# A two-layer streaming encoder on one core: the kernel lays out its own instruction order, and the merge computes a group's factors at once

## The chip, the core and the metric

The kernel runs on one core of a Trainium2 chip. The metric is device time in microseconds (us) for one execution, and lower is better. The core has a matmul engine (PE, whose weight loads are listed as PEld), a vector engine (DVE), a scalar and activation engine (ACT), a general engine (POOL), and a queue that issues transfers (SP). Each engine takes its own instructions strictly in the order in which the built program lists them; an instruction whose inputs are not there holds back everything listed behind it on that engine.

## What is computed

Two layers, each one sub-layer with four groups of heads fed by one input projection:

```
aq, ak, av, ag, bcq, bckv, bkr, bg, cq, ck, cv, cg, mq, mg = split_in(rms(x) @ w_in)
o_a = band attention, 9 chunks of 64, relative bias, softmax
o_b = latent attention (low rank q and kv, rotary), softmax over the past
o_c = stick-breaking attention (sigmoids, reverse cumulative product)
o_m = attention into 256 memory tokens
y   = rms(heads(concat(o_a, o_b, o_c, o_m))) * out_g * silu(gates)
x   = x + y @ w_out
```

The prompt has 2048 frames of 1024 channels; a second input of 64 frames goes through the same layers with caches. All of it is float32.

## The kernel before

The 2048 frames are 16 tiles of 128 rows, and the sample is a 17th. They are worked in three blocks of 6, 6 and 5 tiles. Two streams of work are written as Python generators. The projection stream (`p_stream`) multiplies tiles by chunks of 256 weight columns: float32 operands are split into a high and a low part, and three matmuls per 128 rows of the contraction are summed (lines 404, 405 and 407, tile `pp`, from `xh`, `xl` and the weight pieces `wh`). A weight piece arrives by a transfer (`raw`), and POOL (line 306) and DVE (line 307) split it. The attention stream (`attention`) goes through units of one head and up to two query tiles: scores into `ps` (lines 857, 858, 860), a mask or a maximum on DVE, exponentials or sigmoids on ACT, for group C a scan on DVE (line 1104) and a product on POOL (line 1106), then transposes of the weights `s` into `pt` on PE (line 902), a split of `pt` into `ph` by ACT (line 905) and DVE (line 138), and the products `ot` with the values on PE (line 927). At the end `os`, `ob` and `opark` bring the output back to rows (lines 933, 943, 949).

The main loop at the end of `hybrid_step` decides, by a table of costs and due points (`target`), which of the two generators speaks next. That fixes the order in which instructions are written. It does not fix the order in which they run: the kernel is built in a context with `schedule_with_timeline_sim=True`, where the framework collects the written instructions, gives each tile one of the slots of its pool, and lists the instructions on each engine in an order of its own, by its own timing of them. On-chip sums share few slots: `pp` has two, the pool `ps_st` (for `ps`, `pt`, `ob` and the other transposes) five, `ot` one.

`merge` ends a group of one block. It takes the parked outputs `opark` (six tiles of 128 rows by four heads of 64) and works tile by tile: a square on ACT (line 1335), a sum over each head on DVE (line 1337), then for groups A, B and M a reciprocal of the softmax sums, two products and a scale-and-add on DVE (lines 1344 to 1347), a power of -0.5 on POOL (`rpow`, line 141, on 128x4 numbers), a product with the reciprocal on DVE (line 1351), the product with the output on DVE (line 1352), the product with the gate on POOL (line 1354), and a transfer to `Y`. For group C the small rows are one scale-and-add (line 1340) and the power. The output projection of the block reads `Y`.

```
            V.reciprocal(out=st[:, 1], in_=rs)
            V.tensor_tensor(out=st[:, 0], in0=st[:, 0], in1=st[:, 1], op=ALU.mult)
            V.tensor_tensor(out=st[:, 0], in0=st[:, 0], in1=st[:, 1], op=ALU.mult)
            V.tensor_scalar(out=st[:, 0], in0=st[:, 0], scalar1=1.0 / HD, scalar2=EPS, op0=ALU.mult, op1=ALU.add)
            rpow(st[:, 2], st[:, 0], nh)
```

Of the kernel before, what the change touches and what calls it, by code (L numbers as in the profile page):

```python
# [16 lines left out]
NH = 4  # L17
# [27 lines left out]

class PsumPool:
# [18 lines left out]
def hybrid_step(  # L65
# [15 lines left out]
    V, A, G, T = nc.vector, nc.scalar, nc.gpsimd, nc.tensor  # L81
# [18 lines left out]
    nc.sync.dma_start(out=ident_f[:, 0:128], in_=c_ident)  # L100
# [7 lines left out]
    def masks():  # L108
        for dst, src, w in ((bmask, c_bmask, 512), (spad, c_spad, 256)):
            raw = pj.tile([128, 512], F32, tag="kv", name="raw5", bufs=1)  # L110
            nc.sync.dma_start(out=raw[:, 0:w], in_=src)
            V.tensor_copy(dst, raw[:, 0:w])
        tri_f = pj.tile([128, 2, 128], F32, tag="nrm", name="tri_f", bufs=2)
        nc.sync.dma_start(out=tri_f[:, 0], in_=c_tri)
        nc.sync.dma_start(out=tri_f[:, 1], in_=c_stri)
# [52 lines left out]
    def layer_consts(l):  # L168
# [4 lines left out]
        nc.sync.dma_start(out=gc, in_=gcol[l])  # L173
        gr = lay.tile([128, NGAIN], F32, tag="gr", name="gr", bufs=1)
        nc.sync.dma_start(out=gr, in_=grow[l:l + 1, :].to_broadcast([128, NGAIN]))
# [6 lines left out]
        nc.sync.dma_start(out=qg, in_=qcol[l])  # L182
# [5 lines left out]
    def layer_weights(l):  # L188
# [6 lines left out]
        for k in range(2):  # L195
            raw = pj.tile([128, 512], F32, tag="kv", name="raw5", bufs=1)
            nc.sync.dma_start(out=raw[:, 0:384], in_=w_q[l, k * 128:(k + 1) * 128, :])
# [7 lines left out]
        nc.sync.dma_start(out=raw, in_=w_kv[l])  # L205
# [93 lines left out]
    def weights(job, c0, w, out):  # L299
# [14 lines left out]
        for k in range(0, 8, n):  # L314
            raw = pj.tile([128, n, 256], F32, tag="raw", name="raw", bufs=4)
            nc.sync.dma_start(out=raw[:, :, 0:w], in_=src[:, k:k + n])
# [126 lines left out]
    def folded(fn, w, t, pp, rstd):  # L443
# [8 lines left out]
        nc.sync.dma_start(out=up[:, 0:w], in_=ev[64:128, 0:w])  # L452
# [39 lines left out]
    def k_stack(src, dst, scale=None):  # L492
# [12 lines left out]
        nc.sync.dma_start(out=dst.rearrange("a (i p) t -> p (a i) t", p=128),  # L505
                          in_=kt.bitcast(F32).rearrange("p a i t -> p (a i) t"))

    def qr_stack(src, dst):
# [6 lines left out]
        nc.sync.dma_start(out=dst[0:2].rearrange("a p t -> p a t"), in_=kt.bitcast(F32))  # L515
        nc.sync.dma_start(out=dst[2], in_=kt[:, 0].bitcast(F32))

    def v_stack(src, dst):
# [4 lines left out]
        for a in range(2):  # L523
            nc.sync.dma_start(out=dst[a].rearrange("h p w -> p h w"),
                              in_=vs[64 * a:64 * a + 64].bitcast(F32).rearrange("p h a b -> p h (a b)"))

    def kr_stack(kr, dst):
# [10 lines left out]
        nc.sync.dma_start(out=dst, in_=kt.bitcast(F32))  # L538
# [27 lines left out]
    def load_trig(t):  # L566
        trig = pj.tile([128, 64], F32, tag="trig", name="trig", bufs=4)
        nc.sync.dma_start(out=trig, in_=c_trig[t * 128:(t + 1) * 128, :])
# [17 lines left out]
    def chunk_fns(l, b):  # L586
# [19 lines left out]
        def out_rows(t, prompt, sample, src):  # L606
            if t == SAMP:
                nc.sync.dma_start(out=sample, in_=src[0:64])
            else:
                nc.sync.dma_start(out=prompt, in_=src)  # L610
# [10 lines left out]
        def gate(g):  # L621
            def fn(t, pp, rstd):
# [6 lines left out]
                nc.sync.dma_start(out=d["G" + g, b][:, t - tl[0], :], in_=ev)  # L629
            return fn  # L630

        def ak(t, pp, rstd):
# [5 lines left out]
            if t == SAMP:  # L638
                nc.sync.dma_start(out=o_aks[l, 64:128, :], in_=nf[0:64])
            elif t >= NT - KEEP:  # L640
                nc.sync.dma_start(out=o_akp[l, rows(t - (NT - KEEP)), :], in_=nf)
            k_stack(nf, kdst("A", t))

        def av(t, pp, rstd):
            ev = evict(pp, rstd)
            yield
            if t == SAMP:
                nc.sync.dma_start(out=o_avs[l, 64:128, :], in_=ev[0:64])
# [920 lines left out]
```

## Time and profile before

| | |
|---|---|
| time, median of 3 runs | 3338.14 us (3336.03 to 3340.5) |
| the profiled execution's own time | 3338.43 us |
| its span, first to last instruction | 3336.3 us |
| PE, PEld busy | 3155.7 us (95%), 3012.4 us (90%) |
| DVE, ACT, POOL busy | 2658.4 us (80%), 1942.9 us (58%), 1509.3 us (45%) |
| matmuls | 24486 |
| transfers by the hardware queue | 554.10 MB, 58.7% of 16 engines |

The span is what the profile sees of one execution; its own time is 2.1 us longer. Busy time of an engine is the union of its instructions' durations. Matmuls overlap each other, so a busy PE is not necessarily a PE that issues as fast as it can.

### The profile page before, as it was taken

To read this page: it belongs to the slowest core of one execution; us is meant where nothing else is said; L and a number is where in the kernel's file an instruction comes from. 1 tells how busy PE (TensorE), PEld (TensorE's weight loads), DVE (VectorE), ACT (ScalarE), POOL (GpSimd) and SP (SyncE) were. 2 spreads that over 40 slices of the span, in tenths; PEclk is the share of its full clock that TensorE was granted. 3 is DMA by queue.
4 is the path that set the end of the run, shared out by engine and by line. 5 is a ranking of instruction groups with operands and counts; after the bars stand their busy time and mean duration, and the time that the engine had idled before them with its cause. 6 is when DMAs were issued, how large, how long until landed. Compare 5 with 4: busy or idle time off the path is not lost.

```text
span 3336.3 us, 75730 instructions
## 1 busy us (share of the span) xinstructions
PE 3155.7 (95%) x24486; PEld 3012.4 (90%) x24486; DVE 2658.4 (80%) x7977; ACT 1942.9 (58%) x5336; POOL 1509.3 (45%) x2353
## 2 busy tenths in 40 slices
PE   8999899999999998999999889999999999999998
PEld 7899899899998998999999788989998998989897
DVE  5686768999787689887777977799878888877984
ACT  4456645677665556565556765666646566654651
POOL 4554445566345246442434534466414444102553
PEclk9999999999999999999999999999999999999999
DMA  7655776545657666465566567654445766556644
GB/s 203 173 158 159 209 199 186 145 118 145 173 143 200 185 185 180 140 179 162 143 190 183 158 172 215 188 145 122 135 138 164 211 189 185 159 151 184 167 114 145
DMA packets 576122, 558.94 MB, mean 168 GB/s; under 512 B 70960, under 2 KB 478000, under 8 KB 575728
## 3 DMA queue, kind: packets, MB, share of 16 engines
q1 hardware_dynamic: 575728, 554.10, 58.7%
q8 instruction: 196, 3.21, 0.4%
q14 instruction: 198, 1.62, 0.2%
HBM read 378.21 MB, written 173.75 MB: 165 GB/s over the span
## 4 chain that ended last, share of the span: by engine, by line
PE 55%; DVE 18%; DMA 13%; issue 5%; ACT 4%; POOL 3%; SPq 2%; POOLq 0%; ACTq 0%; DVEq 0%
PE pp L405 10%; PE pp L404 10%; PE pp L407 9%; PE ot L927 6%; PE pt L902 6%; DVE wh L307 5%; DVE r L1104 3%; PE ps L857 3%; PE ps L858 3%; DVE ph L138 3%; PE ps L860 2%; PE ob L943 1%; DMA y<-y 1%; PE ptx L261 1%; PE ptk L496 1%
## 5 line engine op out<-in xcount | busy, mean ns | idle before, releaser
L405 PE MATMUL pp<-wh,xh 128*128 128x256 f32 x4416 | 1262.4, 290 | 14.1 <-DVE wh L307 13.5
L404 PE MATMUL pp<-wh,xh 128*128 128x256 f32 x4416 | 1256.5, 290 | 15.2 <-ACT ev L439 10.5
L407 PE MATMUL pp<-wh,xl 128*128 128x256 f32 (+1 forms) x4416 | 1245.9, 284 | 1.3 <-DVE xl L138 1.3
L405 PEld LDWEIGHTS pp<-wh,xh 128*128 128x128 f32 x4416 | 837.9, 190 | 37.7 <-DVE wh L307 25.3
L404 PEld LDWEIGHTS pp<-wh,xh 128*128 128x128 f32 x4416 | 834.4, 190 | 31.3 <-ACT ev L439 13.7
L407 PEld LDWEIGHTS pp<-wh,xl 128*128 128x128 f32 x4416 | 840.3, 191 | 11.8 <-DVE xl L138 2.3
L306 POOL TENSOR_SCALAR wh<-raw,gc 128x256 fp32r<-128x256 f32 (+1 forms) x848 | 470.4, 570 | 323.8 <-PE pp L407 160.2
L927 PE MATMUL ot<-ph,kv 128*128 128x256 f32 (+1 forms) x3104 | 588.9, 293 | 24.4 <-DVE ph L138 11.1
L905 ACT CAST ph<-pt 128x512 fp32r<-128x512 f32 (+2 forms) x840 | 450.7, 551 | 248.9 <-PE pt L902 233.7
L138 DVE TENSOR_TENSOR ph<-pt,ph 128x512 fp32r<-128x512 f32 (+2 forms) x840 | 525.9, 633 | 70.7 <-ACT ph L905 66.8
L902 PE MATMUL pt<-identr,s 128*128 128x128 f32 x3056 | 507.7, 275 | 24.2 <-ACT s L1001 7.8
L927 PEld LDWEIGHTS ot<-ph,kv 128*128 128x128 f32 x3104 | 454.4, 189 | 45.5 <-DVE ph L138 20.1
L307 DVE SCALAR_TENSOR_TENSOR wh<-raw,gc,wh 128x256 fp32r<-128x256 f32 (+1 forms) x848 | 467.6, 576 | 19.4 <-POOL wh L306 18.6
L1106 POOL TENSOR_TENSOR s<-s,r 128x512 f32<-128x512 f32 (+3 forms) x328 | 323.9, 988 | 343.0 <-DVE r L1104 293.6
L857 PE MATMUL ps<-kv,qbuf 128*128 128x512 f32 (+3 forms) x1024 | 377.2, 371 | 25.5 <-DVE r L1104 13.1
L902 PEld LDWEIGHTS pt<-identr,s 128*128 128x128 f32 x3056 | 360.0, 141 | 42.5 <-ACT s L1001 12.1
L141 POOL TENSOR_TENSOR st<-st,mhalf 128x4 f32<-128x4 f32 (+1 forms) x312 | 277.5, 896 | 256.0 <-DVE st L465 218.3
L1104 DVE TENSOR_TENSOR_SCAN r<-ps,r,one 128x512 f32<-128x512 f32 (+3 forms) x328 | 360.0, 1104 | 30.8 <-ACT ps L1097 28.4
L858 PE MATMUL ps<-kv,qbuf 128*128 128x512 f32 (+3 forms) x1024 | 350.5, 344 | 0.0
L439 ACT ACTIVATE ev<-pp,xst 128x256 f32<-128x256 f32 (+1 forms) x424 | 198.5, 470 | 160.0 <-PE pp L407 120.6
L1053 ACT ACTIVATE s<-s,nm 128x512 f32<-128x512 f32 (+3 forms) x328 | 212.6, 651 | 112.5 <-DVE nm L1045 66.0
L1094 ACT ACTIVATE s<-ps 128x512 f32<-128x512 f32 (+3 forms) x328 | 175.1, 534 | 145.7 <-DVE ps L1092 93.8
(172 smaller groups left out, 5072.7 us busy)
## 6 DMA issues: line engine op xcount, KB each, us to landing
raw<-in_w_in SPq DMA_DIRECT2D x288, 256.0 KB, 3.6
kv<-kvC SPq DMA_DIRECT2D x128, 256.0 KB, 4.2
kv<-kvB SPq DMA_DIRECT2D x128, 256.0 KB, 4.2
kv<-kvA SPq DMA_DIRECT2D x96, 256.0 KB, 4.4
raw<-in_w_out SPq DMA_DIRECT2D x96, 256.0 KB, 3.6
y<-y SPq DMA_DIRECT2D x136, 128.0 KB, 2.7
xin<-y SPq DMA_DIRECT2D x64, 256.0 KB, 3.9
qC<-kt SPq DMA_DIRECT2D x34, 256.0 KB, 2.7
```

Source lines behind the costliest of these rows:

```text
L138: (eng or V).tensor_tensor(out=dst, in0=src, in1=hi.bitcast(F32), op=ALU.subtract)
L306: G.tensor_scalar(out=h, in0=raw, scalar1=gc[:, k:k + 1], scalar2=1.0, op0=ALU.mult, op1=ALU.mult)
L307: V.scalar_tensor_tensor(out=lo, in0=raw, scalar=gc[:, k:k + 1], in1=h.bitcast(F32), op0=ALU.mult, op1=ALU.subtract)
L404: T.matmul(pp, lhsT=xh[:, k], rhs=wh, start=(k == 0), stop=False)
L405: T.matmul(pp, lhsT=xh[:, k], rhs=wl, start=False, stop=end)
L407: T.matmul(pp[:, 0:w], lhsT=xl[:, k], rhs=wh, start=False, stop=(k == 7))
L857: T.matmul(ps[:, 0:w], lhsT=q[:, 0, qs], rhs=kt[:, c0:c0 + w], start=True, stop=False)
L858: T.matmul(ps[:, 0:w], lhsT=q[:, 1, qs], rhs=kt[:, c0:c0 + w], start=False, stop=(qr is None))
L902: T.transpose(pt[:, (u + x) * 128:(u + x + 1) * 128], self.p_of(i, j), ident)
L905: A.copy(out=ph[:, 0:w], in_=pt[:, 0:w])
L927: T.matmul(ot[:, e * lo, il[0]:il[0] + n], lhsT=p["vt"](j), rhs=phl[:, e, u * 128:(u + n) * 128], start=start and e == 0, stop=stop and e ...
L1104: V.tensor_tensor_scan(r[:, 0:w][:, ::-1], cc[:, ::-1], one.to_broadcast([128, w]), r[:, w:w + 1], ALU.mult, ALU.min)
```

## The change

A class `Plan` stands between the kernel and the engines. Every call of an engine (and every transfer, now called through `Y`) is only recorded, in the order in which it was written, with the parts of tiles that it reads and writes. From these `Plan.add` finds what each instruction depends on. At the end `plan.issue` goes through all of them in a simulated time of its own: each engine takes, whenever it is free, the ready instruction that was written first, with a charge for its duration by kind and size (`cost`), a charge for the way from one engine to another (`LAG`), a charge for a change of the activation table, and with the pools' slots handed out in the order in which tiles were created. The instructions are then issued in the order of their simulated starts, in a context (`tc.manual_schedule()`) in which the framework keeps that order on each engine. The arithmetic, the tiles and the slot counts stay, but for the merge.

`merge` now has two passes over the tiles of a group: first all squares and sums, into one tile of 128 x (4 x 6 x 4), then the small rows once for all tiles (128x24, or 128x20 in the last block), and then the products, gates and transfers tile by tile.

```
+class Plan:
+    LAG = {"PE": 160, "DVE": 100, "ACT": 100, "POOL": 150, "SP": 200}
...
+        n = cols(outs[0])
+        if eng == "PE":
+            if method == "transpose" or kw.get("rhs") is None:
+                return 110, 271
+            n = cols(kw["rhs"])
+            return max(0.46 * n + 1, 110), 170 + 0.53 * n
+        if eng == "SP":
+            size = 4 * outs[0].shape[0] * n if len(outs[0].shape) > 1 else 4 * n
+            return 530, 2800 + size * 0.0072
+        if eng == "DVE":
+            if method == "tensor_tensor_scan":
+                d = 150 + 2.2 * n
+            elif n <= 16:
+                d = 185 + (cols(ins[0]) if method == "tensor_reduce" else 0) * 0.85
+            elif len(ins) > 1 and sbuf(ins[0]) and sbuf(ins[1]):
+                d = 200 + 1.35 * n
+            else:
+                d = 150 + 1.05 * n
+            return d - 80, d
+        if eng == "ACT":
+            d = 190 + 0.76 * n
...
+        elif kw.get("op") is not None and "pow" in str(kw["op"]):
+            d = 600 if n == 1 else 1050
+        elif method == "tensor_scalar":
+            d = 245 + 1.3 * n
+        else:
+            d = 200 + 1.75 * n
+        return d - 30, d
...
+            for e in ready:
+                while clock[e] <= now and ready[e]:
+                    i = heapq.heappop(ready[e])
+                    key = slot(i)
+                    if key is not None:
+                        parked[key].append(i)
+                        continue
...
+        with tc.manual_schedule():
+            for i in sorted(range(n), key=lambda i: (start[i], i)):
+                op = ops[i]
+                op[1](*op[2], **op[3])
...
-    V, A, G, T = nc.vector, nc.scalar, nc.gpsimd, nc.tensor
+    plan = Plan()
+    V, A, G, T, Y = [plan.engine(n, x) for n, x in (
+        ("DVE", nc.vector), ("ACT", nc.scalar), ("POOL", nc.gpsimd), ("PE", nc.tensor), ("SP", nc.sync))]
...
+        st = at.tile([128, 4, MAXB, NH], F32, tag="mst", name="mst", bufs=2)
         for i0 in range(nq):
+            y = at.tile([128, NH, HD], F32, tag="y", name="y", bufs=2)
+            A.activation(out=y, in_=opark[:, i0], func=ACTF.Square)
+            V.tensor_reduce(out=st[:, 0, i0], in_=y, op=ALU.add, axis=AX.X)
+            if i0 % 2 == 1:
+                yield
+        f0, f1, f2, sc = [st[:, i, 0:nq].rearrange("p q h -> p (q h)") for i in range(4)]
+        if g == "C":
+            V.tensor_scalar(out=f1, in0=f0, scalar1=1.0 / HD, scalar2=EPS, op0=ALU.mult, op1=ALU.add)
+            rpow(sc, f1, nq * nh)
+            yield
+        else:
+            V.reciprocal(out=f1, in_=rspark[:, 0:nq].rearrange("p q h -> p (q h)"))
+            V.tensor_tensor(out=f0, in0=f0, in1=f1, op=ALU.mult)
+            V.tensor_tensor(out=f0, in0=f0, in1=f1, op=ALU.mult)
+            V.tensor_scalar(out=f0, in0=f0, scalar1=1.0 / HD, scalar2=EPS, op0=ALU.mult, op1=ALU.add)
+            rpow(f2, f0, nq * nh)
+            yield
+            V.tensor_tensor(out=sc, in0=f1, in1=f2, op=ALU.mult)
+        for i0 in range(nq):
             gt = at.tile([128, 256], F32, tag="gt", name="gt", bufs=2)
...
+    plan.issue(tc)
```

The order on the engines, at three places. In the changed program every row has the line of `plan.issue`'s call, so the names of the tiles tell what a row is. The first place is DVE in the first layer, at the merge of the first group (C of the first block), before:

```order
L1337 TENSOR_REDUCE mst<-y 128x4 x2
L1340 TENSOR_SCALAR mst<-mst 128x4 x2
L1031 ISA s,mx<-ps,bmask 128x256
L1031 ISA mx 128x1
L1041 TENSOR_SCALAR nm<-mx 128x2
L1352 TENSOR_TENSOR y<-opark,mst 128x256
L627 SCALAR_TENSOR_TENSOR ev<-sg,ev 128x256
L1352 TENSOR_TENSOR y<-opark,mst 128x256
```

and of the changed program, the same merge behind its last sum:

```order
L291 TENSOR_REDUCE mst<-y 128x4 x2
L291 TENSOR_SCALAR mst<-mst 128x24
L291 TENSOR_TENSOR rspark<-rspark,f 128x2
L291 TENSOR_TENSOR rspark<-rspark,rst 128x2
L291 SCALAR_TENSOR_TENSOR ev<-sg,ev 128x256
L291 TENSOR_TENSOR y<-opark,mst 128x256 x2
L291 TENSOR_TENSOR ph<-pt,ph 128x512
```

The scale-and-add that releases the power on POOL, and the product that waits for it, stood once for each pair of tiles; now they stand once for all six, with three rows between them and a split of `ph` behind.

The second place is POOL at the same merge (`mst` with `mhalf` is the power, `wh` a weight piece), before:

```order
L141 TENSOR_TENSOR mst<-mst,mhalf 128x4 x2
L1354 TENSOR_TENSOR y<-y,gt 128x256 x2
L306 TENSOR_SCALAR wh<-raw,gc 128x256 x8
L141 TENSOR_TENSOR mst<-mst,mhalf 128x4 x2
L1354 TENSOR_TENSOR y<-y,gt 128x256 x2
```

and now:

```order
L291 TENSOR_SCALAR wh<-raw,gc 128x256 x8
L291 TENSOR_TENSOR mst<-mst,mhalf 128x24
L291 TENSOR_TENSOR y<-y,gt 128x256 x2
L291 TENSOR_SCALAR wh<-raw,gc 128x256 x8
L291 TENSOR_TENSOR y<-y,gt 128x256 x2
```

Three pairs of 128x4 powers became one of 128x24, and eight weight pieces that stood behind the first pair stand ahead of it.

The third place is PE in the second layer, group B of the second block, from the last transpose of a `pt` to the first product with the `ph` made from it, before:

```order
L902 MATMUL pt<-identr,s 128x128
L927 MATMUL ot<-ph,kv 128x256 x4
L943 MATMUL ob<-identr,os 128x128
L857 MATMUL ps<-kv,qbuf_89 128x512
L858 MATMUL ps<-kv,qbuf_89 128x512
L860 MATMUL ps<-kr,qr 128x512
L857 MATMUL ps<-kv,qbuf_89 128x512
L858 MATMUL ps<-kv,qbuf_89 128x512
L860 MATMUL ps<-kr,qr 128x512
L902 MATMUL pt<-identr,s 128x128 x2
L927 MATMUL ot<-ph,kv 128x256
```

and now:

```order
L291 MATMUL pt<-identr,s 128x128
L291 MATMUL ps<-kr,qr 128x512
L291 MATMUL ot<-ph,kv 128x256 x3
L291 MATMUL ps<-kv,qbuf_85 128x512 x2
L291 MATMUL ps<-kr,qr 128x512
L291 MATMUL pp<-wh,xh 128x256
L291 MATMUL ot<-ph,kv 128x256
```

Between the transpose and the product that needs its split stood 13 matmuls, and now stand eight.

## Rows read from the trace of the kernel before

**Rows 1.** The page: busy time of each engine, and the granted clock in 40 slices.
```profile
PE 3155.7 (95%) x24486; PEld 3012.4 (90%) x24486; DVE 2658.4 (80%) x7977; ACT 1942.9 (58%) x5336; POOL 1509.3 (45%) x2353
...
PEclk9999999999999999999999999999999999999999
```
**Rows 2.** Busy us by stretch: stretch, length, PE, PEld, DVE, ACT, POOL, clock, DMA, GB/s.
```profile
0.00:100.00 100.00, 82.61 (x589) 78.17 (x590) 55.60 (x190) 41.82 (x116) 43.66 (x96) 0.97 0.70 201
...
600.00:900.00 300.00, 287.17 (x2200) 271.22 (x2201) 271.08 (x671) 202.94 (x516) 169.28 (x253) 1.00 0.50 141
...
3200.00:3336.00 136.00, 120.64 (x951) 115.64 (x949) 81.27 (x162) 37.82 (x84) 53.69 (x79) 0.98 0.44 134
sum 3336.00, PE 3155.75 PEld 3012.37 DVE 2658.43 ACT 1942.95 POOL 1509.31; mean PE 242.75 PEld 231.72 DVE 204.49 ACT 149.46 POOL 116.10
```
**Rows 3.** Timeline of PE, a dense piece: start us, us, engine line operation.
```profile
1553.67 0.28 PE L405 MATMUL pp<-wh,xh 128*128 128x256 f32 x1
1553.79 0.28 PE L407 MATMUL pp<-wh,xl 128*128 128x256 f32 x1
1553.91 0.28 PE L404 MATMUL pp<-wh,xh 128*128 128x256 f32 x1
...
1556.23 0.40 PE L857 MATMUL ps<-kv,qbuf 128*128 128x512 f32 x1
1556.47 0.39 PE L858 MATMUL ps<-kv,qbuf 128*128 128x512 f32 x1
```
**Rows 4.** Groups of PE by form: xcount | busy us, mean ns | idle before, releasers.
```profile
L405 PE MATMUL pp<-wh,xh 128*128 128x256 f32 x4416 | 1262.4, 290 | 14.1 <-DVE wh L307 13.5
```
**Rows 5.** Waits of PE: who waited for whom, us in total, times, longest us.
```profile
PE pp L405 <- DVE wh L307: 13.5, 30, 1.6
PE ps L857 <- DVE r L1104: 13.1, 21, 2.1
...
PE ot L927 <- DVE ph L138: 11.1, 15, 2.1
...
PE pp L404 <- ACT ev L439: 10.5, 14, 2.5
...
PE pp L404 <- DVE fo L431: 0.2, 1, 0.2
```
**Rows 6.** Waits of all engines, the merge's power on POOL.
```profile
POOL mst L141 <- DVE mst L1347: 187.0, 36, 71.9
```
**Rows 7.** Groups of POOL by form.
```profile
L306 POOL TENSOR_SCALAR wh<-raw,gc 128x256 fp32r<-128x256 f32 x800 | 448.8, 577 | 307.3 <-PE pp L407 159.2 <-PE pp L405 101.8 <-issue 36.2
...
L141 POOL TENSOR_TENSOR st<-st,mhalf 128x4 f32<-128x4 f32 x210 | 220.4, 1052 | 182.1 <-DVE st L465 148.7 <-DVE mst L1346 8.5 <-DVE f L1048 5.0
L141 POOL TENSOR_TENSOR mst<-mst,mhalf 128x4 f32<-128x4 f32 x136 | 140.3, 1038 | 239.8 <-DVE mst L1347 187.0 <-DVE mst L1340 46.9 <-DVE nm L1041 3.8
...
L141 POOL TENSOR_TENSOR st<-st,mhalf 128x1 f32<-128x1 f32 x102 | 57.7, 573 | 73.9 <-DVE st L465 69.5 <-DVE rspark L1066 3.4 <-DVE nm L1041 0.2
```
**Rows 8.** Groups of DVE by form.
```profile
L138 DVE TENSOR_TENSOR ph<-pt,ph 128x512 fp32r<-128x512 f32 x616 | 416.2, 681 | 58.8 <-ACT ph L905 55.4
L1104 DVE TENSOR_TENSOR_SCAN r<-ps,r,one 128x512 f32<-128x512 f32 x224 | 283.4, 1273 | 16.4 <-ACT ps L1097 15.8
...
L1351 DVE TENSOR_TENSOR mst<-mst 128x4 f32<-128x4 f32 x102 | 23.4, 229 | 8.7 <-POOL mst L141 7.6 <-POOL r L1101 0.7
...
L1344 DVE RECIPROCAL mst<-rspark 128x4 f32<-128x4 f32 x102 | 17.0, 167 | 2.4 <-ACT s L1001 2.2
```
**Rows 9.** Groups of ACT by form.
```profile
L905 ACT CAST ph<-pt 128x512 fp32r<-128x512 f32 x616 | 354.1, 588 | 173.5 <-PE pt L902 168.5 <-PE ot L927 3.1
```
**Rows 10.** Timeline of all engines near the end: a split of `ph` handed from ACT to DVE.
```profile
3247.93 0.37 ACT L905 CAST ph<-pt 128x256 fp32r<-128x256 f32 x1 [1.67 <-DVE ph L138]
...
3248.33 0.42 DVE L138 TENSOR_TENSOR ph<-pt,ph 128x256 fp32r<-128x256 f32 x1
```
**Rows 11.** Timeline of all engines at a merge: DVE's rows, and PE's pause.
```profile
1236.19 1.05 DVE L1351 TENSOR_TENSOR mst<-mst 128x4 f32<-128x4 f32 x1
...
1237.28 0.67 DVE L1352 TENSOR_TENSOR y<-opark,mst 128x256 f32<-128x256 f32 x1
1237.87 0.68 DVE L138 TENSOR_TENSOR ph<-pt,ph 128x512 fp32r<-128x512 f32 x1
...
1238.61 0.74 PE L927 MATMUL ot<-ph,kv 128*128 128x256 f32 x4 [2.08 <-DVE ph L138]
```
**Rows 12.** Transfers of the page: KB each, median us from issue to landing.
```profile
kv<-kvC SPq DMA_DIRECT2D x128, 256.0 KB, 4.2
...
y<-y SPq DMA_DIRECT2D x136, 128.0 KB, 2.7
xin<-y SPq DMA_DIRECT2D x64, 256.0 KB, 3.9
```
**Rows 13.** Timeline at the last merge: PE's first transposes of the last projection, DVE's last output.
```profile
3255.46 1.03 PE L261 MATMUL ptx<-identr,xin 128*128 128x128 f32 x8
...
3255.91 0.23 DVE L949 TENSOR_TENSOR opark<-ob,opark 128x64 f32<-128x64 f32 x1 [0.76 <-ACT opark L948]
```

More of the change, by code (lines that the diff above doesn't have):

```diff
@@ L99, in hybrid_step @@
     ident_f = pj.tile([128, 256], F32, tag="ev", name="ident_f", bufs=3)
-    nc.sync.dma_start(out=ident_f[:, 0:128], in_=c_ident)
+    Y.dma_start(out=ident_f[:, 0:128], in_=c_ident)
     identr = const.tile([128, 128], F32R, name="identr")
@@ L204, in layer_weights @@
         raw = pj.tile([128, 512], F32, tag="kv", name="raw5", bufs=1)
-        nc.sync.dma_start(out=raw, in_=w_kv[l])
+        Y.dma_start(out=raw, in_=w_kv[l])
         copy_r(wkh, raw)
@@ L315, in weights @@
             raw = pj.tile([128, n, 256], F32, tag="raw", name="raw", bufs=4)
-            nc.sync.dma_start(out=raw[:, :, 0:w], in_=src[:, k:k + n])
+            Y.dma_start(out=raw[:, :, 0:w], in_=src[:, k:k + n])
             raws.append(raw)
@@ L451, in folded @@
         up = pj.tile([64, 256], F32, tag="up", name="up", bufs=1)
-        nc.sync.dma_start(out=up[:, 0:w], in_=ev[64:128, 0:w])
+        Y.dma_start(out=up[:, 0:w], in_=ev[64:128, 0:w])
         yield
@@ L537, in kr_stack @@
         A.copy(out=kt, in_=pt)
-        nc.sync.dma_start(out=dst, in_=kt.bitcast(F32))
+        Y.dma_start(out=dst, in_=kt.bitcast(F32))
     def small_T(src, n, tag):
@@ L567, in load_trig @@
         trig = pj.tile([128, 64], F32, tag="trig", name="trig", bufs=4)
-        nc.sync.dma_start(out=trig, in_=c_trig[t * 128:(t + 1) * 128, :])
+        Y.dma_start(out=trig, in_=c_trig[t * 128:(t + 1) * 128, :])
         return trig
@@ L607, in out_rows @@
             if t == SAMP:
-                nc.sync.dma_start(out=sample, in_=src[0:64])
+                Y.dma_start(out=sample, in_=src[0:64])
             else:
-                nc.sync.dma_start(out=prompt, in_=src)
+                Y.dma_start(out=prompt, in_=src)
         def q_norm(g):
@@ L628, in fn @@
                 yield
-                nc.sync.dma_start(out=d["G" + g, b][:, t - tl[0], :], in_=ev)
+                Y.dma_start(out=d["G" + g, b][:, t - tl[0], :], in_=ev)
             return fn
@@ L638, in ak @@
             if t == SAMP:
-                nc.sync.dma_start(out=o_aks[l, 64:128, :], in_=nf[0:64])
+                Y.dma_start(out=o_aks[l, 64:128, :], in_=nf[0:64])
             elif t >= NT - KEEP:
-                nc.sync.dma_start(out=o_akp[l, rows(t - (NT - KEEP)), :], in_=nf)
+                Y.dma_start(out=o_akp[l, rows(t - (NT - KEEP)), :], in_=nf)
             k_stack(nf, kdst("A", t))
@@ L647, in av @@
             if t == SAMP:
-                nc.sync.dma_start(out=o_avs[l, 64:128, :], in_=ev[0:64])
+                Y.dma_start(out=o_avs[l, 64:128, :], in_=ev[0:64])
             elif t >= NT - KEEP:
-                nc.sync.dma_start(out=o_avp[l, rows(t - (NT - KEEP)), :], in_=ev)
+                Y.dma_start(out=o_avp[l, rows(t - (NT - KEEP)), :], in_=ev)
             v_stack(heads(ev), vdst("A", t))
@@ L754, in f @@
             def f(x, q):
-                nc.sync.dma_start(out=x, in_=mem[i * 128:(i + 1) * 128, q * 512:(q + 1) * 512])
+                Y.dma_start(out=x, in_=mem[i * 128:(i + 1) * 128, q * 512:(q + 1) * 512])
             return f
@@ L768, in mv @@
             yield
-            nc.sync.dma_start(out=o_mvp[l, i * 128:(i + 1) * 128, :], in_=ev)
+            Y.dma_start(out=o_mvp[l, i * 128:(i + 1) * 128, :], in_=ev)
             v_stack(heads(ev), kv_part(d, "M", 1, i))
@@ L780, in load @@
             ev = pj.tile([128, 256], F32, tag="ev", name="ev", bufs=3)
-            nc.sync.dma_start(out=ev[:, 0:w], in_=src)
+            Y.dma_start(out=ev[:, 0:w], in_=src)
             return ev
@@ L1332, in merge @@
+        for i0 in range(nq):
             gt = at.tile([128, 256], F32, tag="gt", name="gt", bufs=2)
[L1333 removed]
+            Y.dma_start(out=gt, in_=d["G" + g, b][:, i0, :])
             y = at.tile([128, NH, HD], F32, tag="y", name="y", bufs=2)
[L1335 to L1337 removed]
```

273 lines of the change are left out of this document (219 added, 54 removed).

## The prediction

> **What bounds the kernel now.** I read the page first. PE is busy for 3155.7 of 3336.3 us, and its granted clock is 90% or more of the upper of its two levels, 2.4 GHz, in every slice [rows 1]; so the kernel is bound by PE, and what a change of order can give is the time in which PE does not issue. The page shows 3336.3 - 3155.7 = 180.6 us of it directly. DVE comes next with 80%, and in the stretch from 600 to 900 us with 271 of 300 us, next to PE's 287 [rows 2].
>
> Then I asked how dense a dense piece of PE is. In the timeline, matmuls of 256 columns follow each other every 0.12 us and those of 512 every 0.24 us [rows 3], while the group's mean duration is 290 ns [rows 4]: each overlaps the next ones, and busy time still counts the last 290 - 120 = 170 ns before every pause. The waits of PE are 63 kinds of 169.2 us in 224 pauses, the largest 13.5 us and the last 0.2 us [rows 5]. With the hidden tails the pauses cost 180.6 + 224 x 0.17 = 219 us. Of the idle time 17.4 us lie in the first 100 us and 15.4 us in the last 136 us [rows 2], where loads fill and the last projection drains. I leave these 33 us alone, and 186 us remain that a better order could reach.
>
> No kind dominates. Two of the four listed are data that come late (`wh`, `ph`: 24.6 us), the other two slots that a reader gives back late (the scan's `ps`, the eviction of `pp`: 23.6 us) [rows 5]. That is what it looks like when engines that work strictly in their listed order get a list that doesn't fit the durations of the chip. The plainest sign is POOL, which stood 187 us, once 71.9 us at a stretch, in front of the merge's power because it was listed long before DVE came to its input [rows 6].
>
> **The change part by part.**
>
> *The order.* Nothing that PE computes is added or removed: 24486 matmuls before and after. What counts is whether the planner's time is that of the chip. Its charges are, for the large kinds, within 2% of the rows: 119 ns against 0.12 us for a matmul of 256 columns [rows 3], 578 against 577 ns for a weight piece on POOL [rows 7], 688 against 681 ns for a split and 1276 against 1273 ns for a scan on DVE [rows 8], 579 against 588 ns for a cast [rows 9]. Ways between engines are charged above what they take: ACT to DVE 100 ns where the row shows 30 [rows 10], DVE to PE 160 where it shows 60 [rows 11]. A half of `kv` is charged 4.69 us where the median is 4.2 [rows 12]. So what PE waits for comes mostly a little earlier than planned. How much of the 186 us goes cannot be read from any row. It is bounded by nothing (every pause is a slot that stays full) and by all of it; a loss, with new pauses, is the first rival below. I take 70%, nearer to the upper end because data waits are half of the listed ones and many slots come free late only because their reader on DVE or ACT is listed late: **-130 us**.
>
> *The merge's small rows on DVE.* Outside group C there were 102 of each of five kinds, now 18: 84 x 5 rows of 167 to 229 ns [rows 8] are some 84 us of DVE. I cost them at nothing. PE is the bound, and DVE falls from 80 to about 77%; if PE became so dense that DVE were level with it, the 84 us would be part of what makes the 70% possible.
>
> *The power on POOL.* 136 of 1038 ns become 24, of 24 columns (16 times) or 20 (8 times). A power of one column takes 573 ns, of four 1052 [rows 7]: 160 ns a column over 413 ns. At that slope 24 columns take 4.25 us and 20 take 3.6; the ends are 1.05 us, if the width costs nothing, and 6.3 us, if it is six times four. I take the slope, since both rows lie on it. POOL then spends 97 us instead of 141, but the planner charges 1.05 us whatever the width, so each power ends about 3 us after its plan. Behind it on DVE stands the product that needs it: in the built order 1 to 21 rows lie between the scale-and-add and that product, five or fewer in 14 of the 24 merges, at most some 1.8 us of cover. DVE then stands for 4.25 - 1.8 = 2.5 us, with splits of `ph` queued behind it, in 14 places: 35 us. The row at 1237 us shows the way of it today: the merge's rows stand ahead of a split on DVE, and PE pauses 2.08 us for that split [rows 11]. PE has projection matmuls listed between, so I pass on half: **+18 us**, between 0 and 60. On POOL itself weight pieces or group C's products stand behind some powers; they are late by the same 3 us and are within this bound.
>
> By the Trainium skill (GPSIMD Engine Reference, 3.1, Elementwise) an operation with two inputs costs about 2.6 cycles per element on POOL, so that the width would be almost free; as an estimate from that page the power would stay near 1.1 us, this term would be nothing, and the sum 18 us lower. The rows speak against it for a power: three more columns cost 479 ns [rows 7].
>
> *Chains with little cover.* From the last transpose of a `pt` to the product with its `ph` PE has work listed; by the spacing of rows 3 it is under 1.7 us for 98 of the 840 in the new order, for 26 in the old. The chain itself takes 588 + 30 + 681 + 60 ns = 1.36 us [rows 8 to 11] and the transposes' own tail. So up to 72 more chains fall short by up to 0.4 us, at most 29 us. The planner could have put projection work there if any had been ready; many of them lie in the last block's group C. I take **+8 us**.
>
> *The last merge.* The sums of all five tiles come before the one power. From the last output at 3256 us [rows 13] the way is a square, a sum, 3.6 us of power, a product, the gate, 2.7 us of writing and 3.9 us of reading [rows 12], together some 12.5 us, so the last projection can start near 3269; before, its first transposes came at 3255.5 [rows 13]. Covered or not depends on the projection that is left over: in the new order the last attention product stands 220 matmuls (26 us at 0.12) earlier in PE's list, which is cover enough. I take **+5 us**, between 0 and 13.
>
> *SP and transfers.* The same transfers go out, in planned order too. A store that waits for a late result holds the loads behind it, as now. I count no gain and no loss.
>
> **Sum.** 3338.4 (the profiled execution, 0.3 us over the median of the runs) - 130 + 18 + 8 + 5 = **3239 us**.
>
> **The rivals.**
>
> *Slower: every chain pays.* The planner gives PE an attention product as soon as its inputs should be ready. If on the chip DVE is late for the splits as a rule, because its rows stretch while POOL works (the merge's product took 1.05 us at 1236 us against a mean of 229 ns [rows 8, 11]), PE pays at each of the 840. At 0.25 us each that is 210 us; even with all of the 186 us gone, and the other terms' 31 us, the result is 3338 - 186 + 210 + 31 = 3393. It is slower from 0.18 us a chain on. For it speaks the shorter cover in the third place of the order, eight matmuls instead of 13; against it, that the planner's charges leave the chain some 0.27 us more than the rows take. Chance 0.11.
>
> *No change: the slots are full.* Five slots for `ps`, `pt` and `ob`, two for `pp`, one for `ot` are what they were. If PE's pauses are times in which no slot is free in any order, they come back elsewhere: 3338. The Trainium skill (Perfetto Trace Analysis, Optimization Strategy) says that the same gap repeating on the engine that should be saturated can mean too few buffers; by that rule an order gives nothing. The trace bears it out for about half of the listed waits, and no single gap repeats: 63 kinds share 169 us [rows 5]. Chance 0.06, with the case that a small gain is just eaten by the power.
>
> *Nearly all pauses go.* If 95% go and the width of the power costs nothing, it is 3338 - 177 + 5 = 3166; with 85% it is 3338 - 158 + 5 = 3185. Chance 0.2.
>
> *The change does not do what it says.* The built program's order differs on every engine in the way the change describes, so this gets no chance of its own.
>
> **How the numbers follow.** My own case, with 50 to 85% of the pauses gone, has 0.48 and by itself lies between 3200 and 3275. A smaller gain (5 to 50%, or the bounds of the other terms at their worst) has 0.15, up to 3331. With the third rival that makes 0.83 for faster by over 0.2% (6.7 us, about what a measurement of this kernel can tell from no change), 0.06 for no change, 0.11 for slower. The range runs from 3165, where nearly all of the third rival is in, to 3330; left out are no change and slower, 0.17.
>
> **What would show it.** PE idle on the page at 90 to 130 us instead of 180.6, and the waits view with fewer than 150 pauses. POOL's group of the 128x24 power at 4.2 us, and DVE waiting for it in some 14 merges. POOL no longer standing for tens of us in front of a merge. The forecast is wrong if the power shows 1 us (then the sum is 18 us too high), if `ot` waiting for `ph` grows to more than 100 us (the first rival), or if waits for slots keep their sum while the others vanish (the second).

## The result, and the profile after

The changed kernel takes **3284.4 us** (median; 3282.2 to 3298.25) where the kernel before took 3339.3 beside it: a ratio of 0.9845, 95% interval 0.9817 to 0.9874, so 1.3 to 1.8% faster. In microseconds that is -52 by the ratio and -55 by the medians, where the forecast was 3239, -99.

First the page of the changed kernel, which answers to [rows 1]: busy time and granted clock.

```profile
PE 3144.2 (96%) x24486; PEld 3007.0 (92%) x24486; DVE 2623.8 (80%) x7529; ACT 1954.2 (60%) x5336; POOL 1467.9 (45%) x2241
...
PEclk9999999999999999999999999999999999999999
```

The span is 3281.8 us, so PE's idle time went from 180.6 to 137.6 us, and 11.5 us of its busy time went too. The hidden tails of the prediction, 0.17 us behind each of the 62 pauses that are gone, would be 10.5 of them. The clock is as before, 0.992 of its upper level on average against 0.991. DVE lost 34.6 us of busy time, not 84: neighbouring rows overlap ([rows 11]: the split at 1237.87 starts 0.08 us before the product ahead of it ends), so a short row that goes frees less than its duration.

Next the waits of PE, changed kernel (who waited for whom, us in total, times, longest us), for [rows 5]:

```profile
PE pp L291 <- DVE wh L291: 11.3, 27, 0.9
PE ptx L291 <- DMA xin<-in_x_prompt: 9.7, 5, 6.5
PE pp L291 <- ACT ev L291: 9.2, 8, 4.0
PE ot L291 <- DVE ph L291: 8.0, 9, 1.8
PE pt L291 <- POOL s L291: 6.2, 8, 1.8
PE ps L291 <- DVE r L291: 6.1, 12, 1.1
...
PE ot L291 <- DVE r L291: 0.2, 1, 0.2
```

59 kinds share 124.8 us in 162 pauses; before it was 63, 169.2 and 224. The four kinds listed there all shrank, the scan's most (13.1 to 6.1). What has grown is the fifth row, where PE waits for a product on POOL: 6.2 us, before 1.1 in two pauses. All of PE's waits for POOL rose from 3.6 to 12.7 us.

The merge's power, groups by form on POOL, DVE and ACT of the changed kernel, for [rows 7], [rows 8] and [rows 9] (xcount | busy us, mean ns | idle before, releasers):

```profile
L291 POOL TENSOR_TENSOR st<-st,mhalf 128x4 f32<-128x4 f32 x210 | 224.0, 1069 | 206.1 <-DVE st L291 171.2 <-DVE nm L291 25.4 <-DVE f L291 4.3
...
L291 POOL TENSOR_TENSOR mst<-mst,mhalf 128x24 f32<-128x24 f32 x16 | 66.9, 4182 | 70.2 <-DVE mst L291 70.2
L291 POOL TENSOR_TENSOR st<-st,mhalf 128x1 f32<-128x1 f32 x102 | 57.5, 572 | 99.3 <-DVE st L291 67.1 <-DVE nm L291 21.3 <-DVE rspark L291 10.4
...
L291 POOL TENSOR_TENSOR mst<-mst,mhalf 128x20 f32<-128x20 f32 x8 | 28.3, 3539 | 27.4 <-DVE mst L291 22.1 <-DMA y_p<-xr 4.6 <-DVE r L291 0.7
```
```profile
L291 DVE TENSOR_TENSOR ph<-pt,ph 128x512 fp32r<-128x512 f32 x616 | 413.7, 682 | 110.4 <-ACT ph L291 107.5
L291 DVE TENSOR_TENSOR_SCAN r<-ps,r,one 128x512 f32<-128x512 f32 x224 | 280.8, 1269 | 20.2 <-ACT ps L291 19.6
```
```profile
L291 ACT CAST ph<-pt 128x512 fp32r<-128x512 f32 x616 | 355.8, 588 | 200.8 <-PE pt L291 193.6 <-DVE xr L291 2.9 <-DVE r L291 0.7
```

The power of 24 columns takes 4.18 us, of 20 columns 3.54: the slope of 160 ns a column, which gives 4.25 and 3.61, holds to about 2% far outside the two widths from which it came. Splits, scans and casts cost what they did. And DVE stands for the power, in the waits of all engines, for [rows 6]:

```profile
POOL mst L291 <- DVE mst L291: 92.3, 16, 24.2
...
DVE mst L291 <- POOL mst L291: 35.3, 15, 3.1
...
DVE y L291 <- POOL mst L291: 8.1, 4, 2.7
```

Where the pauses went by stretch, windows of the kernel before and then of the changed one (stretch, length, PE, PEld, DVE, ACT, POOL, clock, DMA, GB/s), beside [rows 2]:

```profile
0.00:600.00 600.00, 559.84 (x4395) 541.85 (x4396) 428.01 (x1361) 319.76 (x929) 300.68 (x521) 0.99 0.65 185
600.00:3000.00 2400.00, 2288.25 (x17719) 2177.95 (x17720) 1979.90 (x6048) 1472.23 (x4064) 1069.21 (x1634) 0.99 0.59 165
3000.00:3400.00 400.00, 307.66 (x2375) 292.56 (x2373) 250.51 (x568) 150.96 (x344) 139.43 (x198) 0.98 0.45 128
```
```profile
0.00:600.00 600.00, 561.83 (x4371) 539.50 (x4372) 434.67 (x1314) 326.10 (x942) 301.20 (x507) 0.99 0.66 185
600.00:3000.00 2400.00, 2316.17 (x18062) 2216.48 (x18061) 1976.32 (x5796) 1498.53 (x4107) 1038.96 (x1559) 0.99 0.60 169
3000.00:3400.00 400.00, 266.22 (x2057) 251.01 (x2055) 212.82 (x421) 129.54 (x289) 127.74 (x176) 0.99 0.37 105
```

PE's idle time is the length less the first number (in the last stretch, what is left of the span). It goes from 40.2 to 38.2 us in the first 600 us, from 111.7 to 83.8 in the middle, and from 28.6 to 15.6 at the end (336.3 - 307.7 and 281.8 - 266.2). The start hardly gained. (The stretches are cut by time, and the faster kernel is a little further on at each cut.) The waits of PE in the first 600 us of the changed kernel begin so:

```profile
PE ptx L291 <- DMA xin<-in_x_prompt: 9.7, 5, 6.5
PE pp L291 <- ACT ev L291: 8.4, 6, 4.0
```

At the other end, the last projection's first transposes, for [rows 13], in PE's timeline:

```profile
3199.03 0.49 PE L291 MATMUL ptx<-identr,xin 128*128 128x128 f32 x3
...
3206.34 0.60 PE L291 MATMUL ptx<-identr,xin 128*128 128x128 f32 x4
```

They carry no bracket: PE did not stand in front of them, as it had projection matmuls to issue.

### The profile page after: what moved, and what is told of

The parts are those of the page before. It is cut to its first block, busy times and chain, and to the rows that moved or that the text cites. A ratio compares the mean times of both kernels' runs of the same rounds, so it can differ in the third digit from the quotient of the medians.

```text
span 3281.8 us, 75026 instructions
## 1 busy us (share of the span) xinstructions
PE 3144.2 (96%) x24486; PEld 3007.0 (92%) x24486; DVE 2623.8 (80%) x7529; ACT 1954.2 (60%) x5336; POOL 1467.9 (45%) x2241
## 5 line engine op out<-in xcount | busy, mean ns | idle before, releaser
L291 PE MATMUL pp<-wh,xh 128*128 128x256 f32 (+1 forms) x9104 | 1811.1, 292 | 29.1 <-DVE wh L291 11.3
L291 PEld LDWEIGHTS pp<-wh,xh 128*128 128x128 f32 x9104 | 1439.2, 190 | 69.1 <-DVE wh L291 26.4
L291 PE MATMUL ot<-ph,kv 128*128 128x256 f32 (+1 forms) x3232 | 577.1, 289 | 14.4 <-DVE ph L291 8.0
L291 PE MATMUL ps<-kv,qbuf 128*128 128x256 f32 (+3 forms) x2048 | 543.5, 361 | 25.8 <-DVE r L291 6.1
L291 ACT ACTIVATE s<-s,nm 128x512 f32<-128x512 f32 (+4 forms) x600 | 383.9, 642 | 189.1 <-DVE nm L291 181.7
L291 DVE SCALAR_TENSOR_TENSOR wh<-raw,gc,wh 128x256 fp32r<-128x256 f32 (+1 forms) x848 | 476.5, 596 | 24.8 <-POOL wh L291 24.2
L291 PEld LDWEIGHTS ot<-ph,kv 128*128 128x128 f32 x3232 | 463.6, 190 | 29.1 <-DVE ph L291 11.6
L291 PEld LDWEIGHTS ps<-kv,qbuf 128*128 128x128 f32 x2048 | 321.5, 190 | 54.9 <-DVE r L291 11.0
L291 ACT ACTIVATE s<-ps 128x512 f32<-128x512 f32 (+3 forms) x328 | 166.1, 538 | 99.8 <-DVE ps L291 56.7
L291 DVE TENSOR_SCALAR_CACHE_REDUCE s<-ps 128x512 f32<-128x512 f32 (+1 forms) x328 | 181.5, 573 | 29.3 <-PE ps L291 28.8
L291 ACT COPY os<-ot 128x256 f32<-128x256 f32 (+1 forms) x384 | 139.4, 363 | 97.1 <-PE ot L291 95.0
```

What stands on the lines that cost most here:

```text
L291: op[1](*op[2], **op[3])
```

## The experiments

The theories. **A**: the term for the wide power was right, and the planner, which charges 1.05 us for it, sets rows behind it too early. **B**, in the first four runs: DVE's stops are covered, and what is missing is missing in the order itself. **S, D, P**, and B in the last run: ways in which the order could give less than 70%, namely, one for each, slots of `wh`, rows that run late against the plan, the choice of the oldest ready row, and banks of PSUM. **C**: the batched merge is itself worth something. Every kernel below is compared with the kernel before on its own chip, by the ratio; the first four shared one chip.

### The changed kernel again

No edit.

> The changed kernel once more, on the chip of the next three, so that they can be set against it. Both theories: 3280 to 3290 us, 0.981 to 0.987 of the kernel before.

Measured: 3288.5 us, 0.9849 (0.9829 to 0.9869). The result stands, and this is the value that the next three are set against.

### The power charged by its rows

```
-            d = 600 if n == 1 else 1050
+            d = 413 + 160 * n
```

> The plan charges the power 413 + 160 n ns for n columns (4.25 us for 24, 3.6 us for 20, 1.05 us for 4) instead of 1.05 us; nothing else differs. Theory A (the term of 18 us for the power is right: DVE's stops behind the power reach TensorE): the 35.3 us for which DVE waits behind the power fall below 8 us, and the time falls by 10 to 18 us against the changed kernel. Theory B (the pauses that stayed come from the order itself; DVE's stops are covered by what the cores of the pipeline hold ready): DVE's waits fall all the same, and the time stays within 5 us of the changed kernel.

Measured: 3263.9 us, 0.9769 (0.9749 to 0.9789). One line of the planner gives 24.6 us against the changed kernel, more than A's 10 to 18, and B's "within 5" falls. From the waits of this kernel:

```profile
DVE mst L291 <- POOL mst L291: 4.5, 4, 3.0
...
DVE y L291 <- POOL mst L291: 3.8, 3, 2.3
```

DVE's stops went from 35.3 + 8.1 to 8.3 us in all, while the power itself is as long as it was (4185 ns). How a stop reached PE is to be seen in the changed kernel. Timeline at 2124 us, all engines (start us, us, engine line operation, in brackets the idle time before and its end):

```profile
2124.07 4.16 POOL L291 TENSOR_TENSOR mst<-mst,mhalf 128x24 f32<-128x24 f32 x1
...
2128.26 0.18 DVE L291 TENSOR_TENSOR mst<-mst 128x24 f32<-128x24 f32 x1 [2.57 <-POOL mst L291]
...
2130.06 0.69 DVE L291 TENSOR_TENSOR ph<-pt,ph 128x512 fp32r<-128x512 f32 x1
...
2130.80 0.63 PE L291 MATMUL ot<-ph,kv 128*128 128x256 f32 x3 [1.77 <-DVE ph L291]
```

DVE stands 2.57 us, a split of `ph` runs after what was held up, and PE stops 1.77 us for it. That is the way that the prediction described. There is a second way, on POOL, at 629 us:

```profile
629.52 4.17 POOL L291 TENSOR_TENSOR mst<-mst,mhalf 128x24 f32<-128x24 f32 x1
...
633.66 1.08 POOL L291 TENSOR_TENSOR s<-s,r 128x512 f32<-128x512 f32 x1
633.72 1.06 DVE L291 TENSOR_TENSOR mst<-mst 128x24 f32<-128x24 f32 x1 [2.48 <-POOL mst L291]
...
634.80 0.55 PE L291 MATMUL pt<-identr,s 128*128 128x128 f32 x3 [1.85 <-POOL s L291]
```

Group C's product `s` stands behind the power on POOL itself, and PE waits for that product, not for DVE. That is the row of PE's waits that grew to 6.2 us; with the true charge it is 3.2. DVE stands for a power over 1 us long in 18 places of the changed kernel; PE pauses within 4 us of the end of 14 of them, 20.3 us in all, by going through the timeline stop by stop. Some of these would have fallen there anyway.

### The order alone, and the merge alone

The first is the changed kernel with the old merge, tile by tile (its loop as in the code before, with `Y.dma_start`, and `mst` in eight slots of 128x4). The second is the kernel before, in the framework's order, with the new merge.

```
-        st = at.tile([128, 4, MAXB, NH], F32, tag="mst", name="mst", bufs=2)
...
+            st = at.tile([128, 4, NH], F32, tag="mst", name="mst", bufs=8)
+            V.tensor_reduce(out=st[:, 0], in_=y, op=ALU.add, axis=AX.X)
...
+                rpow(st[:, 2], st[:, 0], nh)
```

> The changed kernel with the old merge, tile by tile: 136 powers of 4 columns and all small rows of DVE back; order still from the plan. Theory A: without the wide power's stops TensorE's idle time is some 18 us less, the small DVE rows (84 us) cost nothing as they lie under TensorE, so 10 to 23 us below the changed kernel, 3261 to 3275 us. Theory B: within 5 us of the changed kernel. Theory C (the batched merge pays, by the 84 us that DVE is spared): 5 to 20 us above the changed kernel.

> The kernel before, in its old order of issue, with the batched merge alone. Theory A: the power of 3.5 to 4.2 us stands in front of DVE there too: the time is 5 to 30 us above the kernel before. Theory B: within 5 us of it. Theory C: 5 to 25 us below it, since POOL's waits of 187 us in front of 36 powers shrink to 24 powers and DVE has 84 us less to do.

Measured: the order alone 3271.4 us, 0.9785 (0.9765 to 0.9806); the merge alone 3362.0 us, 1.0061 (1.0042 to 1.0080). The order is the whole gain, some 72 us (0.0215 of 3341), and the batched merge took away 17 of them by the medians, 21 by the ratios, in the planned order; alone it costs 20. A's numbers hold both times, but in the merge alone not by A's way, and B and C fall. The middle stretch of the order alone, where PE is idle for 75.2 us:

```profile
600.00:3000.00 2400.00, 2324.80 (x18099) 2226.68 (x18097) 2017.89 (x6176) 1507.75 (x4113) 1069.76 (x1642) 0.99 0.61 170
```

The page and the waits of the merge alone:

```profile
PE 3172.1 (95%) x24486; PEld 3025.3 (90%) x24486; DVE 2620.7 (78%) x7529; ACT 1949.6 (58%) x5336; POOL 1470.4 (44%) x2241
```
```profile
PE ptx L261 <- DMA xin<-y: 19.3, 4, 13.4
...
DVE y L1354 <- POOL mst L141: 3.6, 2, 2.7
DVE mst L1349 <- POOL mst L141: 2.9, 6, 1.2
```

DVE hardly stands for the power (6.5 us, before 10.8). The 13.4 us are the last projection, which waits for the last merge's `y`: from 3200 us on the same wait is 13.8 us, where the kernel before has 4.5, so some 9 us more. But the waits in all did not grow: 171.7 us in 214 pauses, before 169.2 in 224, and PE's idle time in the span of 3355.5 us is 183.4 us, before 180.6. What grew is PE's busy time, by 16.4 us for the same matmuls, and the granted clock is lower: 0.984 on average in this profile, before 0.991; over all runs 0.984 to 0.988, before 0.987 to 0.992. The means of these runs, 0.986 and 0.990, differ by some 13 us of full clock in 3356, so most of the 20 us goes with the clock. The last projection shows it, in PE's timeline at its start and in the stretch from 3279 us on:

```profile
3284.66 1.94 PE L261 MATMUL ptx<-identr,xin 128*128 128x128 f32 x8 [13.41 <-DMA xin<-y]
```
```profile
3279.00:3290.00 11.00, 5.21 (x22) 4.66 (x23) 2.44 (x6) 1.17 (x2) 2.13 (x3) 0.50 0.64 199
```

PE stood for 13.4 us, and the clock was at the lower of its two levels, 0.50, until 3290 us: matmuls of 256 columns started every 0.21 us there, where [rows 3] has 0.12. Why the clock falls more often in this kernel was not tried.

### A ninth slot for the weight pieces

```
-            hl = pj.tile([128, 512], F32R, tag="wh", name="wh", bufs=8)
+            hl = pj.tile([128, 512], F32R, tag="wh", name="wh", bufs=9)
```
(room from `bq` 3 to 2, `trig` 4 to 2, `st` 16 to 10). This edit, and those of the next two sections, are made in the kernel with the mended charge.

> As the kernel with the mended charge of the power (3263.9 us), with a ninth slot for the split weights wh in place of eight; the room comes from slots that are seldom all taken (bq 3 to 2, trig 4 to 2, st 16 to 10). Theory S (the pauses that stayed are work that waits for a slot): 8 to 18 us below, POOL's wait for wh behind PE smaller. Theory D (the pauses that stayed are places where the chip's rows run longer than the plan charges): within 5 us. Theory P (TensorE's ready list is taken in the order of recording, so that projection matmuls that nothing waits for go ahead of the scores, transposes and outputs on which DVE and ACT wait): within 5 us.

Measured: 3270.5 us, 0.9789 (0.9771 to 0.9807), against 0.9769. No gain; S falls for this slot, unless the slots of `bq`, `trig` and `st` that it was paid with cost as much, which was not tried by itself.

### Projections last

```
+        pr = [i + (1000 if ops[i][0] == "PE" and ops[i][5][0].startswith("pp") else 0) for i in range(n)]
...
-                heapq.heappush(ready[ops[i][0]], i)
+                heapq.heappush(ready[ops[i][0]], (pr[i], i))
```

> As the kernel with the mended charge of the power (3263.9 us), but in the plan a projection matmul (pp) that is ready stands 1000 places later in TensorE's ready list, so that a ready score, transpose or attention output goes first and the projection fills the rest. Theory P: 8 to 25 us below, with TensorE's waits for DVE ph and ACT s down by a third or more. Theory S: within 5 us, as the slots are the same. Theory D: within 5 us, or above by up to 10 if the projections then come late.

Measured: 3302.9 us, 0.9881 (0.9866 to 0.9897): 39 us slower. P falls, with its sign, and neither S nor D had allowed for so much. Waits of this kernel:

```profile
DVE wh L292 <- POOL wh L292: 55.4, 85, 2.8
...
DVE ph L292 <- ACT ph L292: 45.2, 71, 3.6
```

With the mended charge alone these are 27.6 and 123.2 us. The attention chain does run with less standing on DVE, as meant, but the weight pieces are now made at the last moment, and DVE stands twice as long for POOL's half of them. How PE loses 39 us by it is not shown: its wait of `pp` for `wh` is 8.9 us, before 8.1, all its waits are 129.2 us, before 114.0, and its busy time is 3158.0 us, before 3136.8. The order of recording, which spreads the projections, is worth keeping.

### Charges by the rows, and the handoff's margin

Edits of the planner's numbers: DVE and POOL charged as the trace has them; 150 ns more lag (below), then 300 ns more; and a shorter lag of 55, 30 and 80 ns for DVE, ACT and POOL.

```
-                d = 200 + 1.35 * n
+                d = (250 if method == "scalar_tensor_tensor" else 125) + 1.35 * n
...
-            d = 200 + 1.75 * n
+            d = 230 + 1.75 * n if n > 256 else 250 + 2 * n
```
```
-    LAG = {"PE": 160, "DVE": 100, "ACT": 100, "POOL": 150, "SP": 200}
+    LAG = {"PE": 160, "DVE": 250, "ACT": 250, "POOL": 300, "SP": 200}
```

The table is read with the engine of the instruction that waits, `j`:

```
                        heapq.heappush(events, (now + (10 if ops[j][0] == e else self.LAG[ops[j][0]]), 2, e, j))
```

So these are charges for the way to DVE, ACT and POOL, and not, as the expectations say, behind them. The way to PE is charged 160 ns in every run, where [rows 11] shows 60; and the shorter lag is no plan without margin.

> As the kernel with the mended charge of the power (3263.9 us), with DVE and POOL charged by the rows: 250 + 1.35 n ns for scalar_tensor_tensor from SBUF (596 for 256 columns, where the trace has 594 for wh and the plan charged 546), 125 + 1.35 n for tensor_tensor (471, where the trace has 470 to 490), POOL's tensor_tensor 762 ns for 256 columns (trace 765, plan 648). Theory D: 8 to 20 us below, the 17 to 21 us of TensorE's pauses before pp behind DVE wh halved. Theories S and P: within 5 us.

> As the kernel with the mended charge of the power (3263.9 us), with 150 ns more between the end of a DVE, ACT or POOL row and its reader on another engine (250, 250, 300 instead of 100, 100, 150), a margin against rows that run late; the handoffs of the trace (31 and 55 ns) are below either. Theory D: 5 to 20 us below, fewer short pauses. Theory S: 5 to 20 us above, as every slot is planned to be held longer. Theory P: 0 to 10 us above.

> As the kernel with the mended charge of the power (3263.9 us), with the handoffs that the trace shows instead of the plan's: 55 ns behind DVE, 30 behind ACT, 80 behind POOL (before 100, 100, 150). Theory D: a plan without margin, 5 to 15 us above 3263.9. Theory S, or that true charges give the best order: 0 to 10 us below.

> As the kernel with 150 ns more lag (3252.9 us), with 300 ns more: 400 ns behind DVE and ACT, 450 behind POOL. Theory D (a margin in the plan takes up rows that run late on the chip): 0 to 10 us below 3252.9. Theory S (each slot is planned to be held longer): 10 to 30 us above, from this point on.

Measured: measured charges 3266.8 us, 0.9775 (0.9758 to 0.9791); lag 250 **3252.9 us, 0.9736** (0.9719 to 0.9753); the shorter lag 3264.8 us, 0.9766 (0.9753 to 0.9780); lag 400 3256.5 us, 0.9741 (0.9724 to 0.9757). Truer charges for rows give nothing, though D had asked for 8 to 20 us: PE's wait of `pp` for DVE's `wh` stands at 8.0 us, before 8.1 (the 17 to 21 us of the expectation were counted from start to start of PE's rows). The prediction's "within 2%" had left out DVE's `wh`, charged 546 ns where the kernel before has 584, and this run says that it cost nothing that can be seen. A margin on the way to DVE, ACT and POOL gives some 10 us (the intervals at 100 and 250 ns just overlap, 0.9749 to 0.9753), and twice as much no more; with less, the time is that of the plan's own lag, not D's 5 to 15 us above. So D holds for the step from 100 to 250 ns alone, and a margin in front of PE was not tried. That rows run late by amounts which no mean shows, and that slack absorbs some of them, fits this and was not shown by itself. The middle stretch of the lag-250 kernel, 600 to 3000 us:

```profile
600.00:3000.00 2400.00, 2327.95 (x18219) 2234.61 (x18217) 1994.81 (x5845) 1515.88 (x4141) 1045.23 (x1566) 0.99 0.61 171
```

PE is idle there for 72.1 us, after 83.8 in the changed kernel and 111.7 before.

### The old merge with the margin

The old merge in the lag-250 kernel.

> The old merge, tile by tile, in the plan's order with the longer lag of 250, 250 and 300 ns; against 3252.9 us with the batched merge, its power rightly charged. Theory A (the small rows of DVE that batching saves, 84 us, are hidden): within 6 us of 3252.9. Theory C (they are worth something once the power is charged): 6 to 20 us above.

Measured: 3269.0 us, 0.9774 (0.9761 to 0.9787), against 0.9736 with the batched merge: the intervals do not meet, and C holds by 13 us (0.0038 of 3342). The pages of the two, first with the old merge:

```profile
PE 3132.7 (96%) x24486; PEld 3005.6 (92%) x24486; DVE 2669.3 (82%) x7977; ACT 1952.7 (60%) x5336; POOL 1506.9 (46%) x2353
```
```profile
PE 3126.6 (96%) x24486; PEld 2999.4 (92%) x24486; DVE 2623.5 (81%) x7529; ACT 1956.9 (60%) x5336; POOL 1466.9 (45%) x2241
```

The 84 us of rows are 46 us of DVE's time; POOL is spared 40 us as well, and which of the two the 13 us come from was not tried. The comparison at the shorter lag (0.9785 and 0.9769) has the same sign, with intervals that overlap. Once its power is charged, the batched merge is a gain.

### A third bank for the projections' sums

```
-    ps_p = PsumPool(pool("ps_p", bufs=2, space=PS))
-    ps_st = PsumPool(pool("ps_st", bufs=5, space=PS))
+    ps_p = PsumPool(pool("ps_p", bufs=3, space=PS))
+    ps_st = PsumPool(pool("ps_st", bufs=4, space=PS))
```

> As the kernel with 150 ns more lag (3252.9 us, 0.9736 of the kernel before), with the eight banks of PSUM dealt 3, 4, 1 instead of 2, 5, 1: a third bank for the projections' sums (pp), one less for scores and transposes. Theory B (the pauses that stay are the wait of TensorE for a bank that an eviction on ACT or DVE has to free, so that work which is ready cannot be sent ahead): 6 to 20 us below, TensorE's waits of pp for ACT ev and DVE gone. Rival (the score side needs its five banks more than the projections a third): 5 to 20 us above. Theory D (rows that run late, wherever the banks are): within 5 us.

Measured: **3247.7 us, 0.9720** (0.9704 to 0.9736), the lowest of all, but 5 us from the kernel with two banks, inside what the intervals allow. The wait that it aims at went, 10.6 us before the edit, and the start gained. Waits, then the first 600 us:

```profile
PE pp L291 <- ACT ev L291: 2.8, 2, 1.4
```
```profile
0.00:600.00 600.00, 568.48 (x4479) 548.22 (x4480) 446.98 (x1339) 337.99 (x970) 305.18 (x516) 0.99 0.67 188
```

PE idles 31.5 us there, after 36.7 with two banks (563.29 of 600 busy) and 40.2 before the change. Nearly all of that came back as other waits later: the middle stretch has 76.9 us of idle time instead of 72.1. So B holds for that place; as a price for the whole kernel, 5 us where it had asked for 6 to 20, it stays unclear. The granted clock, 0.995 on average over these runs and 0.994 over those with two banks, is worth some 3 of the 5 us.

## Why the prediction came out as it did

The sign, the place of the gain and the price of the new wait were right; one term was too large, by 58 us. The other terms were forecast at +31 together and measured +17 to +21: the power cost more, the chains and the last merge cost nothing, and the small rows gave something back. That took 10 to 14 us off the miss, and it was luck. The result lies outside the prediction's own case, 3200 to 3275 with a chance of 0.48, and in the case of a smaller gain, which had 0.15.

- **The order, -130: the step that failed.** The bound of 186 us was reasonable, the share of 70% was not. The order alone measured -72, or 39%. With the power charged, the margin and the third bank the best version stands at -91 (0.9720), about half of the bound. The argument for the upper end was that data waits are half of the listed ones and that late slots follow late readers. What the runs put in its place: in the middle stretch a quarter of the idle time went in the changed kernel, and a third with the order alone (111.7 to 75.2 us). And the first 600 us behave like the start that the prediction excluded only up to 100 us: their 40 us of idle time stayed at 38, and the first projections wait there for `xin` and for evictions (9.7 and 8.4 us). Of these 40 us 22.8 lie behind the first 100 and so in the 186; at 70% they make 16 of the 58 us, and most of the miss is the middle stretch. The margin got 10 us of the rest, a third bank for `pp` perhaps 5. What holds the 76.9 us that the best version still idles in the middle stretch is open: a slot for `wh`, truer charges and another priority were tried, and none moved the time down.
- **The power, +18: right, a little low.** The duration is 4.18 us against 4.25 forecast, DVE's stops in front of the small product are 35.3 us in 15 places against 35 in 14, and the price is 25 us against the true charge; 17 to 21 us against the old merge is what is left of it after what batching saves. Part of it goes by POOL's own order, which the term named without a price. The Trainium skill's rule (GPSIMD Engine Reference, 3.1, Elementwise), by which the width would cost almost nothing, does not describe this operation: 20 more columns than four cost 3.1 us.
- **The small rows on DVE, nothing: low.** With the power charged the batched merge gave 5 (unclear) to 13 us. DVE is spared 46 us in it and POOL 40, so that the small rows are the reason is likely and not shown by itself.
- **Chains with little cover, +8: nothing seen.** `ot` waits for `ph` 8.0 us, before 11.1. The first rival, in which every chain pays, is out.
- **The last merge, +5: nothing here, but real.** In the changed kernel the last projection's transposes start at 3199.0 us without a wait, as PE had projection matmuls left; in the framework's order the same merge held PE 13.4 us, the upper bound that the prediction gave.
- **The rival of full slots** (and the Trainium skill's sentence on gaps and too few buffers: Perfetto Trace Analysis, Optimization Strategy) is out as "no change". The rule has a part of the remainder at most: one more slot for `wh` gave nothing, a third bank took 7.8 us of `pp`'s waits and perhaps 5 of time, not clear of noise.
- **What would show it.** PE's idle time at 137.6 and 162 pauses lay outside the 90 to 130 and "fewer than 150" that were set for the forecast; the power and DVE's stops lay on theirs. POOL still stands up to 24.2 us in front of a merge, a third of what it was.

## What to carry to other kernels

When idle time of the bounding engine is spread over many kinds of waits, a better order recovers part of it: here two fifths, half after mending, and the first 600 us gave almost nothing until a third bank was added; forecast from the middle stretch alone, and not with most of it. A planner that sets the order must know a row that becomes longer: one wrong charge, 1.05 us for a row of 4.2, took back a third of the gain, though it concerns 24 of the 39592 rows of PE, DVE, ACT and POOL on the page. Check a kernel's own cost table against the rows of the profile after every change of a tile's width, and try some slack on the handoffs: 150 ns more on the way to DVE, ACT and POOL gave some 10 us here. And look at the granted clock before a difference is put down to waits: in the merge alone the waits stayed as they were, and the clock did not.

## What was not expected of the hardware

A power with two operands on POOL costs by the column: 572, 1069, 3539 and 4182 ns for 1, 4, 20 and 24 columns, about 157 ns for each column after the first, where POOL's product of 256 columns takes 766. And a small DVE row can take several times its usual time beside POOL: the product of 24 columns at 633.72 us took 1.06 us next to POOL's product at 633.66, while the median of these rows is 182 ns. Its cause was not tried. A pause of PE can cost more than its length: after the 13.4 us in the merge alone the clock was at its lower level, and matmuls came every 0.21 us instead of 0.12.
